# A two-layer streaming encoder: conditioning matmuls issued four together, and up-projection blocks without overlapping columns

## The chip, the cores and the metric

The kernel runs on one core of one Trainium2 chip. The metric is the device time of one launch, in microseconds. TensorE does the matmuls (PE in the profile, PEld its weight loads), VectorE is DVE, ScalarE is ACT, GpSimd is POOL; SyncE (SP) issues all DMAs of this kernel.

## What is computed

One inference step of a two-layer encoder over 1152 rows (1024 of a prompt and 8 x 16 of samples) of 1024 features. Both layers have attention, a feed-forward part with a causal convolution of width 3, and shifts, scales and gates that come from a condition vector `c`:

```python
sc = jax.nn.silu(c)
for l in range(DEPTH):
    ada = (sc @ w_ada[l] + b_ada[l])[:, None, :]
    sh_m, sc_m, g_m, sh_f, sc_f, g_f = jnp.split(ada, 6, axis=-1)
    h = x * (1 + sc_m) + sh_m
    ...
    x = layer_norm(DEEPNORM_ALPHA * x + (1 + g_m) * mix, ln_g[l, 0], ln_b[l, 0])
    h = x * (1 + sc_f) + sh_f
    f, conv_rows = conv_ffn(h, None if prompt else state_conv[l], w_up[l], conv_w[l], conv_b[l], w_down[l])
    ...
    x = layer_norm(DEEPNORM_ALPHA * x + (1 + g_f) * f, ln_g[l, 1], ln_b[l, 1])
```

```python
def conv_ffn(h, prev, w_up, conv_w, conv_b, w_down):
    u = h @ w_up
    ...
    ue = jnp.concatenate([prev.astype(u.dtype), u], axis=1)
    y = conv_b
    for tap in range(CONV_W):
        y = y + conv_w[tap] * ue[:, tap:tap + T]
    a, g = jnp.split(y, 2, axis=-1)
    out = (jax.nn.gelu(g) * a) @ w_down
    return out, ue[:, T:]
```

The convolution goes over positions, so each output position needs the up-projection at its own position and at the two before it.

## The kernel before

**Stages.** `build` runs: the first conditioning product (`ada(0, ...)`), attention of layer 0, the output projection, the feed-forward part of layer 0, and the same three for layer 1. In the trace the first attention lies at about 54 to 430 us, feed-forward layer 0 at 535 to 1340, attention of layer 1 to 2040, feed-forward layer 1 at 2130 to the end.

**Precision.** Every large product is made of three: a matrix is split into a high part rounded to the 32-bit format of TensorE's fast matmul (`float32r`) and a low part, the remainder. `split` (L160) makes the high part with a cast and the low part with a subtraction. Weights come through `wload` (L164): a DMA into one of the two staging buffers `ws`, the cast on ScalarE (L151), the subtraction mostly on GpSimd (L162), into one of four weight slots `wh` and `wl`. `mmT` (L262) does 3 x 8 matmuls for one block of columns, first with the low weight part, then twice with the high one.

**The conditioning products.** `ada(gi, ...)` is a generator that makes one of seven slices of the condition. It has eight steps over the 1024 inputs. A step loads two tiles of 128 x 1024 weights and issues four matmuls (L211) that write the four 32-partition groups of one PSUM bank; `j` 0 and 1 read the first tile, `j` 2 and 3 the second. Each has 32 output rows, so it uses 32 of the array's 128 columns. Slice 0 runs by itself at the start. Slices 1 and 2 run in the background of the first attention, where their weights share the two buffers `ws` with the other weights; slices 3 to 6 run in the background of feed-forward layer 0, from a ring of three buffers of the tile `F`. `wload` calls `step`, which advances the generator.

**The feed-forward part.** For each of 22 slices of 128 features and both halves (`gg` 0 for `a`, 1 for `g`) `up` loads a weight and runs `up_block` for three blocks of rows. `up_block` (L1006) projects a block into one of three PSUM banks (`ub`) and calls `conv`: ScalarE makes the last tap with the bias (L976), VectorE adds the two other taps from the same bank (L979), and for samples GpSimd adds what comes from the state (L994). For `gg` 1 the gelu (L1023, ScalarE), the product with the other half (L1025, GpSimd) and a split follow. The blocks overlap, so that a block's bank holds the columns before it that its taps need:

```python
        UB = ((0, 384), (380, 388), (764, 388))
```

`down` (L1030) multiplies the pairs of slices by the down-projection (L1050), from three other banks, and adds into `acc` on VectorE (L1041). `down_last` (L1054) does the last pair, with the last up-projection's six blocks between the row tiles, and hands each row tile to the normalization.

**What sets the order.** The program is recorded in the order of the Python code, and a list scheduler with a timeline of its own then reorders it, engine by engine, by priorities and by what its timeline says is ready. Two neighbours in the code can so be apart on the engine. Inside an engine the order is then fixed, and each instruction waits for the semaphores of what it needs. A wait on PSUM is kept for a whole bank.

Of the kernel before, what the change touches and what calls it, by code (L numbers as in the profile page):

```python
# [20 lines left out]
BLK = ((0, 384), (384, 384), (768, 384))  # L21
# [67 lines left out]
class Trunk:  # L89
# [101 lines left out]
    def ada(self, gi, bank, ring=None, row=None):  # L191
        nc = self.nc
        ring = ring or self.ws
        ps = self.bank(bank)
# [11 lines left out]
        for k in range(8):  # L206
            w = [ring.next() for _ in range(2)]
            for hf in range(2):
                nc.sync.dma_start(w[hf], self.I["adaw"][gi, k, hf])
            for j in range(4):  # L210
                nc.tensor.matmul(  # L211
                    ps[32 * j : 32 * j + 32, :],
                    self.cT[:, k * 32 : k * 32 + 32],
                    w[j // 2][:, (j % 2) * 512 : (j % 2) * 512 + 512],
                    start=k == 0,
                    stop=k == 7,
                    tile_position=(0, 32 * j),
                )
            yield
        if row is None:  # L220
            row = ring.next()
# [721 lines left out]
    def ffn(self, l, xsrc, xdst, affs):  # L943
        nc, I, O, H = self.nc, self.I, self.O, self.H
# [27 lines left out]

        def conv(ps, cc, bi, y):
            w = lambda i: cw[:, cc, i : i + 1]
            off = 0 if bi == 0 else 4
            nc.scalar.activation(y, ps[:, off : off + 384], AF.Identity, bias=w(3), scale=w(2))  # L976

            def tap(o, u, i):
                nc.vector.scalar_tensor_tensor(o, u, w(i), o, op0=ALU.mult, op1=ALU.add)  # L979

            if bi == 0:
                tap(y[:, 1:384], ps[:, 0:383], 1)
                tap(y[:, 2:384], ps[:, 0:382], 0)
            elif bi == 1:
                tap(y, ps[:, 3:387], 1)
                tap(y, ps[:, 2:386], 0)
            else:
                tap(y[:, 0:256], ps[:, 3:259], 1)
                tap(y[:, 0:256], ps[:, 2:258], 0)
                ys = y[:, 256:384].rearrange("p (s q) -> p s q", q=16)  # L990
                us = ps[:, 260:388].rearrange("p (s q) -> p s q", q=16)
# [13 lines left out]

        def up_block(w, j, gg, bi):  # L1006
            cc = j + 22 * gg
            s0, n = UB[bi]
            ps = self.bank(ub.next())
            self.mmT(w, ps, s0, n)  # L1010
            if gg == 0:
                y = ya[bi] = self.ya.next()
            else:
                y = self.yg.next()
            conv(ps, cc, bi, y)
            if bi == 2:
                uo = self.uo[gg].rearrange("p (j s r) -> p j s r", s=9, r=2)
                src = ps[:, 258:402].rearrange("p (s q) -> p s q", q=16)[:, :, 0:2]
                nc.scalar.copy(uo[:, j % 11], src)
# [319 lines left out]
```

## Time and profile before

| | us |
|---|---|
| median of 3 runs | 2995.66 (2993.42 to 2997.04) |
| the profiled execution, its own time | 2989.15 |
| its span, first to last instruction | 2987.3 |
| mean granted TensorE clock in it | 0.984 |
| up-projection and key matmuls, L267 (8208 of them) | 46% of the chain |
| down-projection matmuls, L1050 | 16% of the chain |
| conditioning matmuls, L211 (224, two records each) | 2% of the chain |

The profile is of one execution. "Busy" is the time in which an engine has an instruction in it; matmuls are pipelined and overlap, so the time that one costs is read from the start of one to the start of the next, and not from its length. "The chain of waits" follows the work that ended last back to what released it. The granted clock is a share of TensorE's full clock.

### The profile page before, as it was taken

Reading aid. Unit: us, or ns where it says so; the run is one execution under the profiler, and the core shown is the slowest. Engines: PE = TensorE matmul, PEld = TensorE weight load, DVE = VectorE, ACT = ScalarE, POOL = GpSimd, SP = SyncE. Lnnn points to the kernel's source line nnn. Section 1 sums busy time; section 2 is a strip of 40 time slices with the busy share of each in tenths; the row PEclk is TensorE's granted clock in tenths of the full one; section 3 lists DMA queues with packets and bytes.
Section 4 is the critical chain, followed back from the end, with each engine's and each line's share of the span. In section 5 each row is a group of like instructions: output and inputs, shape, how many; then the busy total and the mean of one; then the engine's idle time right before and its main releaser. Section 6 shows DMA issues by size and latency. Waiting matters only on the chain.

```text
span 2987.3 us, 43224 instructions
## 1 busy us (share of the span) xinstructions
PE 2863.8 (96%) x16582; PEld 2545.5 (85%) x16582; DVE 1537.3 (51%) x3416; ACT 1145.7 (38%) x2432; POOL 908.0 (30%) x661
## 2 busy tenths in 40 slices
PE   7999889999999999999999999989999999999996
PEld 4886668888888898997999888867899999999995
DVE  4365668424444343358412677766724444444468
ACT  3464643332222222224434666662442222222224
POOL 2122332322222222344561121231432222222253
PEclk9999989999999999999999999999999999999998
DMA  8655353722222222212795467673311111111121
GB/s 299 189 150 160 109 151 113 238 81 77 94 81 86 83 72 99 82 64 103 267 309 165 130 152 195 181 226 118 125 50 38 41 43 46 43 41 40 42 84 74
DMA packets 175535, 353.95 MB, mean 118 GB/s; under 512 B 34632, under 2 KB 91784, under 8 KB 174944
## 3 DMA queue, kind: packets, MB, share of 16 engines
q1 hardware_dynamic: 175328, 351.19, 37.0%
q8 instruction: 130, 2.13, 0.3%
q14 instruction: 77, 0.63, 0.1%
HBM read 285.22 MB, written 75.35 MB: 121 GB/s over the span
## 4 chain that ended last, share of the span: by engine, by line
PE 79%; DVE 8%; DMA 6%; ACT 3%; POOL 2%; issue 2%; SPq 0%; DVEq 0%; ACTq 0%; POOLq 0%
PE PS L267 46%; PE PS L1050 16%; PE PS L279 8%; PE PS L552 2%; PE PS L211 2%; PE PS L533 2%; DMA ws<-in_wo_dram 1%; PE PS L507 1%; DMA F<-in_adaw_dram 1%; DVE F L473 1%; PE PS L510 1%; DMA F<-xd 1%; DVE acc L1110 1%; DMA ws<-oN 1%; POOL wl L162 1%
## 5 line engine op out<-in xcount | busy, mean ns | idle before, releaser
L267 PE MATMUL PS<-H,wh 128*128 128x384 f32 (+1 forms) x5472 | 1045.9, 339 | 0.3 <-DVE H L162 0.3
L267 PEld LDWEIGHTS PS<-H,wh 128*128 128x128 f32 x5472 | 966.6, 188 | 17.5 <-issue 7.5
L162 POOL TENSOR_TENSOR wl<-ws,wh 128x1024 fp32r<-128x1024 f32 x167 | 404.8, 2429 | 751.1 <-ACT wh L151 704.0
L979 DVE SCALAR_TENSOR_TENSOR F<-PS,F 128x256 f32<-128x256 f32 (+2 forms) x704 | 352.9, 512 | 535.7 <-ACT F L976 522.5
L267 PE MATMUL PS<-H,wl 128*128 128x384 f32 (+1 forms) x2736 | 565.1, 343 | 19.6 <-POOL wl L162 7.8
L267 PEld LDWEIGHTS PS<-H,wl 128*128 128x128 f32 x2736 | 486.3, 189 | 53.2 <-issue 18.6
L976 ACT ACTIVATE F<-PS,F 128x384 f32<-128x384 f32 x264 | 177.3, 672 | 751.1 <-PE PS L267 749.6
L1050 PE MATMUL PS<-wh,X 128*128 128x512 f32 x1320 | 412.2, 394 | 10.3 <-DVE acc L1041 4.1
L1041 DVE TENSOR_TENSOR acc<-acc,PS 128x512 f32<-128x512 f32 x324 | 221.4, 685 | 271.6 <-PE PS L1050 271.1
L1025 POOL TENSOR_TENSOR F<-F 128x384 f32<-128x384 f32 x132 | 138.0, 1046 | 649.4 <-ACT F L1023 647.5
L1050 PEld LDWEIGHTS PS<-wh,X 128*128 128x128 f32 x1320 | 245.4, 188 | 64.0 <-issue 6.7
L151 ACT CAST wh<-ws 128x1024 fp32r<-128x1024 f32 x174 | 180.0, 1045 | 154.9 <-PE PS L1050 75.3
L1050 PE MATMUL PS<-wl,X 128*128 128x512 f32 x660 | 216.4, 392 | 0.0
L279 PE MATMUL PS<-wh,H 128*128 128x256 f32 (+1 forms) x936 | 172.5, 314 | 6.3 <-DVE H L162 6.0
L279 PEld LDWEIGHTS PS<-wh,H 128*128 128x128 f32 x936 | 137.3, 195 | 17.0 <-DVE H L162 6.8
L1050 PEld LDWEIGHTS PS<-wl,X 128*128 128x128 f32 x660 | 124.1, 188 | 28.1
L589 POOL TENSOR_TENSOR F<-F,x2att 64x512 f32<-64x512 f32 x62 | 79.4, 1280 | 212.8 <-DVE F L564 171.4
L162 DVE TENSOR_TENSOR X<-F,X 128x384 fp32r<-128x384 f32 x110 | 96.9, 881 | 88.7 <-ACT X L151 88.4
L279 PE MATMUL PS<-x1att,H 128*128 128x512 f32 x504 | 131.8, 402 | 4.9 <-ACT x1att L151 2.7
L533 PE MATMUL PS<-C,F 128*128 128x128 f32 x720 | 118.3, 285 | 17.4 <-DVE wh L539 7.5
L1023 ACT ACTIVATE F<-F 128x384 f32<-128x384 f32 x132 | 69.2, 524 | 143.3 <-DVE F L979 129.0
L279 PEld LDWEIGHTS PS<-x1att,H 128*128 128x128 f32 x504 | 94.7, 190 | 27.8 <-ACT x1att L151 3.4
(211 smaller groups left out, 3477.8 us busy)
## 6 DMA issues: line engine op xcount, KB each, us to landing
ws<-in_wup_dram SPq DMA_DIRECT2D x88, 512.0 KB
F<-in_adaw_dram SPq DMA_DIRECT2D x74, 512.0 KB
ws<-in_wdn_dram SPq DMA_DIRECT2D x44, 512.0 KB
ws<-in_adaw_dram SPq DMA_DIRECT2D x32, 512.0 KB
x1att<-kH SPq DMA_DIRECT2D x60, 256.0 KB
xd<-F SPq DMA_DIRECT2D x27, 512.0 KB
F<-xd SPq DMA_DIRECT2D x27, 512.0 KB
vH<-X SPq DMA_DIRECT2D x40, 256.0 KB
```

Source lines behind the costliest of these rows:

```text
L151: nc.scalar.copy(out, in_)
L162: self.eng(el).tensor_sub(lo, src, hi.bitcast(F32))
L267: self.nc.tensor.matmul(out[:, 0:n], w[a][:, k * 128 : k * 128 + 128], H[:, p, k, s0 : s0 + n], start=i == 0, stop=i == 23)
L279: self.nc.tensor.matmul(out[:, 0:n], H[:, p, j * kn + k, t0 : t0 + 128], w[a][:, k * n : k * n + n], start=i == 0, stop=i == 23,)
L533: nc.tensor.transpose(t[:, m * 128 : m * 128 + 128], p[:, (kt - k0) * 128 : (kt - k0) * 128 + 128], self.ident)
L589: self.eng("v" if last else "p").tensor_mul(on[r, q], on[r, q], rb[r, :])
L976: nc.scalar.activation(y, ps[:, off : off + 384], AF.Identity, bias=w(3), scale=w(2))
L979: nc.vector.scalar_tensor_tensor(o, u, w(i), o, op0=ALU.mult, op1=ALU.add)
L1023: nc.scalar.activation(y, y, AF.Gelu_apprx_tanh)
L1025: nc.gpsimd.tensor_mul(a, y, ya[bi])
L1041: nc.vector.tensor_add(row[:, n], row[:, n], ps)
L1050: nc.tensor.matmul(ps, ac[m][p][:, cs], w[m][q][:, n], start=i == 0, stop=i == 5)
```

## The change

It edits two places.

In `ada` the four matmuls of a step are issued, for every slice but the first, in the order 2, 3, 0, 1. The first of them (`lead`) is ordered as before; the other three get a high priority and an instruction that they may only be issued after the lead. The lead reads the second tile.

In the feed-forward part the three blocks no longer overlap (`BLK`: 0, 384 and 768, 384 columns each). The second and third block are written from column 2 of their bank on, and ScalarE then copies the last two columns of the block before, from that block's bank, into columns 0 and 1. The copy stands behind the matmuls in the code. The offsets in `conv` follow.

```diff
-            for j in range(4):
-                nc.tensor.matmul(
...
+            lead = None
+            for j in (2, 3, 0, 1) if gi else (0, 1, 2, 3):
+                with ExitStack() as es:
+                    if lead is not None:
+                        es.enter_context(self.tc.high_priority())
+                        es.enter_context(self.tc.issue_after(lead))
+                    mm = nc.tensor.matmul(
+                        ps[32 * j : 32 * j + 32, :],
+                        self.cT[:, k * 32 : k * 32 + 32],
+                        w[j // 2][:, (j % 2) * 512 : (j % 2) * 512 + 512],
...
+                if gi and lead is None:
+                    lead = mm.ins
...
-            off = 0 if bi == 0 else 4
+            off = 0 if bi == 0 else 2
...
-                tap(y, ps[:, 3:387], 1)
-                tap(y, ps[:, 2:386], 0)
+                tap(y, ps[:, 1:385], 1)
+                tap(y, ps[:, 0:384], 0)
...
-        UB = ((0, 384), (380, 388), (764, 388))
+        halo = {}
...
-            s0, n = UB[bi]
+            s0, n = BLK[bi]
             ps = self.bank(ub.next())
-            self.mmT(w, ps, s0, n)
+            off = 0 if bi == 0 else 2
+            self.mmT(w, ps[:, off:512], s0, n)
+            if bi:
+                nc.scalar.copy(ps[:, 0:2], halo.pop(cc))
+            if bi < 2:
+                halo[cc] = ps[:, off + 382 : off + 384]
```

Line numbers below 200 stay; in the changed program L211 is L216, L267 is L274, L976 is L983, L979's taps are L986, L1019 is L1031, L1023 is L1035, L1050 is L1062, and the new copy is L1020.

The scheduler sees a different program, so the order moves in many places: on TensorE in the first attention and in both feed-forward layers, not in attention of layer 1. Three places follow. In a row stand the line, the operation, the output and input tiles, the output's shape and, behind an x, how many equal instructions follow each other.

TensorE in feed-forward layer 0, at the end of an up-projection and the start of the down-projections, before. `PS<-F,C` are the conditioning matmuls, `PS<-H,wl` and `PS<-H,wh` the up-projection with the low and high weight parts, `PS<-wh,X_73` and `PS<-wl,X_73` the down-projection.

```order
L267 MATMUL PS<-H,wh 128x388 x16
L211 MATMUL PS<-F,C 32x512 x4
L1050 MATMUL PS<-wh,X_73 128x512 x2
...
L1050 MATMUL PS<-wh,X_73 128x512 x2
L211 MATMUL PS<-F,C 32x512 x2
L267 MATMUL PS<-H,wl 128x384 x8
L1050 MATMUL PS<-wh,X_73 128x512 x2
...
L1050 MATMUL PS<-wh,X_73 128x512 x2
L211 MATMUL PS<-F,C 32x512 x2
L267 MATMUL PS<-H,wh 128x384 x9
```

The same place now:

```order
L274 MATMUL PS<-H,wh 128x384 x16
L216 MATMUL PS<-F,C 32x512 x4
L1062 MATMUL PS<-wh,X_73 128x512 x2
...
L1062 MATMUL PS<-wh,X_73 128x512 x2
L274 MATMUL PS<-H,wl 128x384 x8
L274 MATMUL PS<-H,wh 128x384 x6
L1062 MATMUL PS<-wh,X_73 128x512 x2
...
L1062 MATMUL PS<-wh,X_73 128x512 x2
L216 MATMUL PS<-F,C 32x512 x4
L274 MATMUL PS<-H,wh 128x384 x6
```

Two pairs of conditioning matmuls have become one group of four. Over feed-forward layer 0 the 32 steps stood in 38 groups (two of 1, eleven of 2, one of 3, twenty-one of 4, one of 5, two of 6) and stand in 32 groups of 4; in the first attention the 16 steps stood in 25 groups and stand in 19 (thirteen of 4 and six of 2). The second and third blocks of an up-projection have gone from 388 to 384 columns.

ScalarE in feed-forward layer 1, in the stretch of up-projections, before. `F<-PS,F` is the first activation of a block, `F<-F` the gelu, `wh<-ws` a weight's high part, `X_73<-F` that of a product, `F<-PS 128x18` the copy of the rows that go out as state.

```order
L976 ACTIVATE F<-PS,F 128x384
L1023 ACTIVATE F<-F 128x384
L151 CAST x2ffn_17144<-F 128x384
L976 ACTIVATE F<-PS,F 128x384 x2
L151 CAST wh<-ws 128x1024
L1019 COPY F<-PS 128x18
L976 ACTIVATE F<-PS,F 128x384
```

And now:

```order
L983 ACTIVATE F<-PS,F 128x384
L151 CAST x2ffn_17232<-F 128x384
L1020 COPY PS<-PS 128x2
L983 ACTIVATE F<-PS,F 128x384
L1020 COPY PS<-PS 128x2
L151 CAST wh<-ws 128x1024
L983 ACTIVATE F<-PS,F 128x384
L1031 COPY F<-PS 128x18
```

The copies stand ahead of the activations of the second and third block, and the weight cast has come between the third block's copy and its activation.

TensorE in `down_last` of layer 1, before: the last blocks of the last up-projection and the down-projections around them.

```order
L267 MATMUL PS<-H,wh 128x388 x9
L267 MATMUL PS<-H,wl 128x388 x8
L267 MATMUL PS<-H,wh 128x388 x16
L1050 MATMUL PS<-wh,X_73 128x512 x2
L1050 MATMUL PS<-wl,X_73 128x512 x2
L1050 MATMUL PS<-wh,X_73 128x512 x4
```

And now:

```order
L274 MATMUL PS<-H,wh 128x384 x9
L1062 MATMUL PS<-wh,X_73 128x512 x2
L1062 MATMUL PS<-wl,X_73 128x512 x2
L1062 MATMUL PS<-wh,X_73 128x512 x4
...
L1062 MATMUL PS<-wh,X_73 128x512 x2
L274 MATMUL PS<-H,wl 128x384 x8
L274 MATMUL PS<-H,wh 128x384 x16
```

The last block no longer follows its neighbour directly; it stands behind 18 more down-projection matmuls.

More of the change, by code (lines that the diff above doesn't have):

```diff
@@ L209, in ada @@
                 nc.sync.dma_start(w[hf], self.I["adaw"][gi, k, hf])
-            for j in range(4):
[L211 to L218, printed above, removed]
+            lead = None
[8 more added lines that the diff above has]
+                        w[j // 2][:, (j % 2) * 512 : (j % 2) * 512 + 512],
+                        start=k == 0,
+                        stop=k == 7,
+                        tile_position=(0, 32 * j),
+                    )
+                if gi and lead is None:
+                    lead = mm.ins
             yield
@@ L984, in conv @@
             elif bi == 1:
-                tap(y, ps[:, 3:387], 1)
-                tap(y, ps[:, 2:386], 0)
-            else:
-                tap(y[:, 0:256], ps[:, 3:259], 1)
-                tap(y[:, 0:256], ps[:, 2:258], 0)
+                tap(y, ps[:, 1:385], 1)
+                tap(y, ps[:, 0:384], 0)
+            else:
+                tap(y[:, 0:256], ps[:, 1:257], 1)
+                tap(y[:, 0:256], ps[:, 0:256], 0)
                 ys = y[:, 256:384].rearrange("p (s q) -> p s q", q=16)
-                us = ps[:, 260:388].rearrange("p (s q) -> p s q", q=16)
+                us = ps[:, 258:386].rearrange("p (s q) -> p s q", q=16)
                 tap(ys[:, :, 1:16], us[:, :, 0:15], 1)
```

2 lines of the change are left out of this document (1 added, 1 removed).

## The prediction

> **What bounds the kernel now.** I read the page first: the busy shares, then the chain that ended last.
>
> ```profile
> PE 2863.8 (96%) x16582; PEld 2545.5 (85%) x16582; DVE 1537.3 (51%) x3416; ACT 1145.7 (38%) x2432; POOL 908.0 (30%) x661
> ...
> PE 79%; DVE 8%; DMA 6%; ACT 3%; POOL 2%; issue 2%; SPq 0%; DVEq 0%; ACTq 0%; POOLq 0%
> PE PS L267 46%; PE PS L1050 16%; PE PS L279 8%; PE PS L552 2%; PE PS L211 2%; PE PS L533 2%; DMA ws<-in_wo_dram 1%; PE PS L507 1%; DMA F<-in_adaw_dram 1%; DVE F L473 1%; PE PS L510 1%; DMA F<-xd 1%; DVE acc L1110 1%; DMA ws<-oN 1%; POOL wl L162 1%
> ```
>
> TensorE is busy 96% of the span and holds 79% of the chain. Both edited places, the up-projection matmuls (L267) and the conditioning matmuls (L211), stand on that chain. A share over the span is an average, so next comes the table by stretches: the first attention, then the two feed-forward layers.
>
> ```profile
> 110.00:350.00 240.00, 226.95 (x1586) 184.57 (x1584) 151.99 (x525) 146.05 (x446) 59.86 (x61) 0.97 0.48 144
> 535.00:1340.00 805.00, 802.60 (x4236) 715.07 (x4235) 318.20 (x552) 220.87 (x372) 230.91 (x179) 1.00 0.28 94
> 2130.00:2987.30 857.30, 829.53 (x4339) 776.54 (x4337) 408.81 (x716) 258.36 (x436) 266.59 (x190) 0.99 0.16 52
> ```
>
> The columns are PE, PEld, DVE, ACT and POOL busy, then the granted clock, the DMA share and GB/s. In feed-forward layer 0 TensorE is busy 802.60 of 805 us, in layer 1 829.53 of 857.30 (the rest is the output tail), in the first attention 226.95 of 240. So in the feed-forward layers a nanosecond less per matmul is a nanosecond off the end, while ScalarE has 70% to spare.
>
> **The columns.** Of the three blocks of each up-projection, two had 388 columns and now have 384, from 384-aligned starts in H. I price this from two pieces of the chain and four starts in the timeline.
>
> ```profile
> 1466.63 93.95 PE PS L267 x542
> ...
> 2378.44 39.79 PE PS L267 x226
> ```
>
> ```profile
> 2380.04 1.58 PE L267 MATMUL PS<-H,wl 128*128 128x384 f32 x8
> ...
> 2384.23 1.58 PE L267 MATMUL PS<-H,wl 128*128 128x388 f32 x8
> ...
> 2388.48 1.57 PE L267 MATMUL PS<-H,wl 128*128 128x388 f32 x8
> ...
> 2392.72 1.58 PE L267 MATMUL PS<-H,wl 128*128 128x384 f32 x8
> ```
>
> The first piece is the key projection of attention 1. It runs the same function over exactly the blocks that the change will use, all of 384: 93.95 / 542 = 173.3 ns each. The second is a stretch of three up-projections: 39.79 / 226 = 176.1 ns. By the starts, a 384 block after a 388 one takes 4.19 us and the 388 blocks 4.25 and 4.24. There are 2 layers x 44 projections x 72 = 6336 such matmuls: 6336 x 2.72 ns = 17.2 us (by the starts, 88 x (12.68 - 72 x 0.1733) = 88 x 0.20 = 17.6). Bounds: no gain, if writing the output at column 2 of the bank costs what the four columns did, which no row shows; 17.6 above. I take 17.2, since only that output offset differs from the row.
>
> The Trainium skill, "TensorE: Matmul & The Clock Gate", section "Back-to-back issue gap", gives a warm gap of N/2.4 + 2.5 ns, so that four columns would be worth 1.67 ns; as an estimate by that page, 4224 matmuls would save 7.0 us, and the whole sum would come to 19.6 us in place of 29.8. The trace does not agree on the level: it has 173.3 ns at 384 columns where the page's formula has 162.5.
>
> **The conditioning matmuls.** Four matmuls of one step write four different 32-row groups of one bank and run side by side when they stand together. The timeline of layer 0 has them both ways (the trace writes each as two records).
>
> ```profile
> 730.16 1.68 PE L267 MATMUL PS<-H,wl 128*128 128x384 f32 x8
> ...
> 743.03 1.07 PE L211 MATMUL PS<-F,C 128*32 128x512 f32 x8
> 744.03 1.68 PE L267 MATMUL PS<-H,wl 128*128 128x384 f32 x8
> ...
> 762.21 1.05 PE L211 MATMUL PS<-F,C 128*32 128x512 f32 x4
> 763.19 1.66 PE L267 MATMUL PS<-H,wl 128*128 128x384 f32 x8
> ```
>
> ```profile
> 590.53 1.90 PE L211 MATMUL PS<-F,C 128*32 128x512 f32 x10
> 592.36 1.69 PE L267 MATMUL PS<-H,wl 128*128 128x388 f32 x8
> ```
>
> All four hold TensorE for 1.00 us (743.03 to 744.03), two alone for 0.98. So a pair costs what a four costs. What counts is the number of interruptions. One costs 13.87 (730.16 to 744.03, with one) - 12.68 (2380.04 to 2392.72, without) = 1.19 us. In layer 0 the order has 38 groups before and 32 now: 6 x 1.19 = 7.1 us. Three groups had five or six matmuls and took a second pass, 1.83 - 1.00 = 0.83 us: 2.5 us. Together 9.6 us, on an engine without idle time there. The lead of a four now waits for the second weight tile, and the other three stand right behind it; the rows for what such a wait costs are these, of layer 0 and of the first attention:
>
> ```profile
>   DMA F<-in_adaw_dram: 2.4, 1
> ```
>
> ```profile
>   DMA ws<-in_adaw_dram: 4.0, 4
> ```
>
> In layer 0 TensorE waited once, 2.4 us, for the tile that the first step needs; I leave that where it is. In the first attention the 16 steps stood in 25 groups and stand now in 19 (three steps are still split): 6 x 0.98 = 5.9 us of TensorE time, in a stretch with 13 us of idle time in which other waits end last. I take 4 us. SP's queue holds the same DMAs as before; the weight loads (L209) move a few places past the small score and output DMAs and past one query weight. Bounds: a gain of 9.9 (5.9 and all of the 4.0 of DMA waits), and a loss of 10: the two weight buffers `ws` are shared with the query weights, a four holds both until it has run, and if each of 16 steps waited 1.0 us more (the mean of those four waits), 16 - 5.9 would be lost. Queued behind such a lead are the score and transpose matmuls, for which VectorE waits.
>
> **The halo copies.** 176 copies of 2 columns are new on ScalarE, before the first activation (L976) of the second and third block. A copy waits for its own block's last matmul and, for the bank it reads, for the block before.
>
> ```profile
> L976 ACT ACTIVATE F<-PS,F 128x384 f32<-128x384 f32 x264 | 177.3, 672 | 751.1 <-PE PS L267 749.6
> ```
>
> ```profile
> L1019 ACT COPY F<-PS x88: 149/174/243, 551.2 to 2953.2; 128x18 f32<-128x18 f32 x88
> ```
>
> The nearest row for its price is the other small copy out of PSUM (L1019), 0.174 us: 176 x 0.174 = 30.6 us more on ScalarE, which waited 749.6 us for these very matmuls. How long a block keeps its bank is read from the second block of the stretch above, which ends at 2388.48, and from the rows of its neighbours:
>
> ```profile
> 2388.68 0.67 ACT L976 ACTIVATE F<-PS,F 128x384 f32<-128x384 f32 x1 [1.52 <-PE PS L267]
> ```
>
> ```profile
> 2389.38 1.27 DVE L979 SCALAR_TENSOR_TENSOR F<-PS,F 128x384 f32<-128x384 f32 x2
> ```
>
> ```profile
>   DVE F L979: 1.5, 1
> ```
>
> ```profile
> PEld PS L267 <- POOL wl L162: 13.1, 8, 5.0
> ```
>
> The activation starts 0.20 us after the block, and the taps end at 2390.65, 2.2 us after it. With the copy and its hand-over (0.17 + 0.20) that is 2.6 us; TensorE comes back to this bank two blocks later, 8.5 us after. So 5.9 us of slack cover the copy, and I cost it at 0; without cover it would be 30.6 (176 x 0.174). TensorE's waits for the taps were 1.5 us in all of layer 1. Queued behind a waiting copy on ScalarE are the block's own activation, for which VectorE's taps and then GpSimd's product wait, and in places a weight cast (L151), whose lower half GpSimd makes next; for such halves TensorE waited 13.1 us in the whole program, so they mostly come well ahead of their use. One place has less slack: in `down_last` a block goes into the bank from which the block before it takes its halo, so TensorE must wait for that copy, 0.4 us by the numbers above, four times, unless other matmuls stand between. The order puts down-projection matmuls between; I take 1 us of loss, bounds 0 and 2. In the output tail TensorE waits already:
>
> ```profile
> 2954.08 0.73 PE L1050 MATMUL PS<-wh,X 128*128 128x512 f32 x2 [0.89 <-DVE C L1086]
> ...
> 2959.81 0.50 PE L1050 MATMUL PS<-wh,X 128*128 128x512 f32 x1 [2.25 <-DVE C L1086]
> ```
>
> The last up block now stands in the middle of the down-projections there, with 3.1 us of such waits around it. I count neither gain nor loss, up to 3 us each way.
>
> **Sum.** 17.2 + 9.6 + 4 - 1 = 29.8 us. The profiled execution took 2989.15 us (span 2987.3 and 1.85 around it) and becomes 2959.4. The median of the runs shown is 2995.66, 6.5 above it; the same difference gives 2965.9, so 2966.
>
> **Rivals.** (1) *The columns are worth less.* If a matmul's time went with its columns alone, four would be worth 173.3 / 384 x 4 = 1.8 ns, 7.6 us for 4224; then the sum is 20.2 and the time 2975. If the output offset costs as much as it saves, 2983. The Trainium skill, "TensorE: Matmul & The Clock Gate", section "Back-to-back issue gap", speaks for this side, with one cycle a column. For it stands that only one kind of row, at one alignment, shows 173.3. Against it, that row reads the same addresses.
> (2) *The fours wait for their second tile in the first attention*, losing 10 in place of gaining 4: 2980. For it: both `ws` buffers are held, and the DMA share is 0.48 there. Against: 16 steps in 240 us are 15 us apart.
> (3) *Slower: TensorE becomes bound by the halo copy.* If banks come free late because copies stand behind other work on ScalarE, every second and third block waits. It decides from 30.8 / 176 = 0.175 us a block; at 0.37 (the copy and its hand-over) the loss is 65.1 and the time 3030. For it speaks that a copy waits at the head of an in-order queue, against it the 5.9 us of slack.
> (4) *The fours do not run as fours on the chip*, or something slips between: the columns and the loss of 1 stay, 2979.5. The order speaks against it.
>
> **Chances.** The forecast 0.68, rival 1 0.16, rival 2 0.07, rival 3 0.06, rival 4 0.03. The forecast's own range is 2957 to 2975: 2957 with the attention's upper bound and a kinder tail, 2975 with no gain in the attention and both losses full. Rival 1 ends at 2983, rivals 2 and 4 lie below it. So 2954 to 2984. A measurement of this kernel can tell about 0.2%, 6 us, from no change. Faster by more than that: 0.68 + 0.16, 0.05 of rival 2 and 0.02 of rival 4, 0.91. Within it: 0.02 of rival 2, 0.01 each of rivals 3 and 4, 0.04. Slower: 0.05 of rival 3.
>
> **What would show it.** In the profile after: L267 in attention 1 and in the layers at one mean interval, a piece of 226 of them at 39.2 us in place of 39.79; the same starts 4.16 apart. L211 in layer 0 in 32 runs of eight records, each about 1.0 us. L1019's neighbour, the 2-column copy, at 0.17 us x176, and no row of TensorE that waits for it or for L979 beyond 2 us. The prediction is wrong if the interval stays at 176, if L211 shows DMA waits of over 10 us, or if TensorE's idle time in the layers grows by more than 5 us.

## The result, and the profile after

The changed kernel took 3005.91 us (median of 9 runs, 2997.72 to 3010.45), the kernel before on the same chip 2993.79 (9 runs). The ratio is 1.0033, 95% interval 1.0022 to 1.0044: slower by about 10 us, where 2966 was predicted. The profiled execution took 3007.52 us, its span 3005.7, at a mean granted clock of 0.974 in place of 0.984.

The page after, busy shares and the chain that ended last:

```profile
PE 2859.9 (95%) x16582; PEld 2548.1 (85%) x16582; DVE 1563.2 (52%) x3416; ACT 1162.4 (39%) x2608; POOL 904.0 (30%) x661
...
PE 70%; DVE 7%; ACT 3%; DMA 2%; issue 2%; POOL 2%; SPq 0%; DVEq 0%; ACTq 0%; POOLq 0%
```

TensorE is a little less busy in a longer span. The steady stretches show what was predicted of the columns. First a piece of the chain, then four starts from the timeline:

```profile
2391.52 39.37 PE PS L274 x227
```

```profile
2393.30 1.55 PE L274 MATMUL PS<-H,wl 128*128 128x384 f32 x8
...
2397.45 1.55 PE L274 MATMUL PS<-H,wl 128*128 128x384 f32 x8
...
2401.61 1.55 PE L274 MATMUL PS<-H,wl 128*128 128x384 f32 x8
...
2405.78 1.55 PE L274 MATMUL PS<-H,wl 128*128 128x384 f32 x8
```

39.37 / 227 = 173.4 ns, and the blocks start 4.16 us apart: output from column 2 on costs nothing. So the loss lies elsewhere. The table by stretches has the same windows as before:

```profile
110.00:350.00 240.00, 224.04 (x1566) 182.95 (x1565) 149.94 (x514) 142.56 (x437) 59.49 (x61) 0.96 0.47 142
535.00:1340.00 805.00, 799.15 (x4278) 718.21 (x4277) 343.01 (x570) 230.37 (x457) 236.11 (x182) 1.00 0.28 96
2130.00:3005.70 875.70, 837.37 (x4375) 781.61 (x4373) 427.10 (x719) 272.86 (x534) 273.03 (x193) 0.98 0.16 53
```

The last window spans 18 us more, and TensorE is idle 38.3 us in it where it was 27.8. Windows of equal length are too coarse to say where. I therefore cut the execution at the same instructions in each kernel (us from start to start; the kernels in the three columns on the right are experiments that follow):

| stretch | before | changed | old blocks in last slice | old blocks in first two and last | halo by taps |
|---|---|---|---|---|---|
| first output projection to first down-projection, layer 0 | 208.1 | 208.5 | 206.6 | 195.7 | 195.2 |
| from there to the last slice, layer 0 | 767.9 | 754.5 | 754.3 | 759.6 | 758.0 |
| last slice, layer 0 | 61.3 | 73.1 | 64.4 | 64.6 | 68.1 |
| end of output projection to first down-projection, layer 1 | 63.7 | 75.5 | 75.1 | 62.8 | 55.0 |
| from there to the last slice, layer 1 | 728.6 | 719.2 | 719.2 | 723.3 | 729.1 |
| last slice, layer 1 | 53.3 | 66.5 | 54.0 | 55.2 | 57.9 |

The two long stretches gain 13.4 and 9.4. Three short ones give back 11.8, 11.8 and 13.3: the last slice of each layer, and the start of feed-forward layer 1. (Where up- and down-projections are put shifts some time between a start and the stretch behind it, so these two are read together.) By the same cuts, TensorE's idle time in these three grew by 20.7 us, and it lost 11.8 us more to a lower clock; the other 4.4 are mostly work that moved into the start of layer 1 from the stretch behind it. Outside the table the changed kernel loses 6.9 us up to the first output projection, which starts at 396.55 in place of 389.70, and 1.0 in attention of layer 1, and gains 4.0 behind the last matmul.

**The start of feed-forward layer 1.** TensorE before, then after. The first block of a projection is 384 wide in both; H's third block of columns is still being made here.

```profile
2135.46 1.63 PE L267 MATMUL PS<-H,wl 128*128 128x384 f32 x8 [1.52 <-DVE F L979]
2136.93 2.94 PE L267 MATMUL PS<-H,wh 128*128 128x384 f32 x16
2139.70 1.04 PE L867 MATMUL PS<-C,F 128*128 128x128 f32 x8
2140.50 1.66 PE L267 MATMUL PS<-H,wl 128*128 128x388 f32 x8
2142.00 2.99 PE L267 MATMUL PS<-H,wh 128*128 128x388 f32 x16
2144.82 1.58 PE L267 MATMUL PS<-H,wl 128*128 128x384 f32 x8
```

```profile
2142.76 2.34 PE L274 MATMUL PS<-H,wl 128*128 128x384 f32 x8 [1.83 <-ACT PS L1020]
2144.90 3.69 PE L274 MATMUL PS<-H,wh 128*128 128x384 f32 x15
2148.43 1.03 PE L874 MATMUL PS<-C,F 128*128 128x128 f32 x8
2149.22 0.42 PE L274 MATMUL PS<-H,wh 128*128 128x384 f32 x1
2153.52 2.82 PE L274 MATMUL PS<-H,wl 128*128 128x384 f32 x8 [3.88 <-ACT H L151]
```

Before, five blocks stand ahead of the first that needs H's third part: two of the first projection, two of the second (2135.46 and 2140.50), one of a third (2144.82). After, three do. The second block of the second projection would go into the bank that holds the halo for the third block of the first. That copy (L1020) stands behind the third block's matmuls, which wait for H. So nothing is left to put there, and TensorE waits 3.88 us for the cast of H. The wait of 1.83 us ahead of it was 1.52 before, for the taps alone.

The waits cost more than their length. The granted clock is the third number from the end of a row in the table by windows:

```profile
2142.00:2143.00 1.00, 0.23 (x1) 0.27 (x2) 0.90 (x5) 0.49 (x2) 0.00 (x0) 1.00 0.00 0
2143.00:2144.00 1.00, 1.00 (x6) 1.00 (x6) 1.00 (x2) 0.33 (x1) 0.12 (x1) 0.71 0.09 16
2144.00:2145.00 1.00, 1.00 (x5) 1.00 (x4) 0.94 (x2) 0.00 (x0) 1.00 (x1) 0.50 0.00 0
2145.00:2146.00 1.00, 1.00 (x5) 1.00 (x4) 0.00 (x0) 0.00 (x0) 1.00 (x1) 0.50 0.00 0
2146.00:2147.00 1.00, 1.00 (x5) 1.00 (x4) 0.72 (x1) 0.00 (x0) 0.25 (x1) 0.58 0.00 0
```

Behind the wait the clock is halved for some 3.4 us: 0.29 + 0.50 + 0.50 + 0.42 = 1.71 us lost. The transposes at 2148.43, on which the cast of H depends, come later by that. The Trainium skill, "TensorE: Matmul & The Clock Gate", section "What's actually happening", has a window of 3413 ns, and half the rate after one that was idle. The trace agrees with the length and the rate, but no whole idle window was needed here: a wait of 1.83 us was enough.

**The last slice.** A block goes here into the bank from which the block before it takes its halo. The second blocks, in layer 0 after, on ScalarE and then on TensorE:

```profile
1372.23 0.52 ACT L1035 ACTIVATE F<-F 128x384 f32<-128x384 f32 x1 [0.60 <-DVE F L986]
1374.16 0.51 ACT L151 CAST X<-F 128x384 fp32r<-128x384 f32 x1 [1.40 <-POOL F L1037]
1374.57 0.15 ACT L1020 COPY PS<-PS 128x2 f32<-128x2 f32 x1
```

```profile
1374.78 2.43 PE L274 MATMUL PS<-H,wl 128*128 128x384 f32 x8 [3.28 <-ACT PS L1020]
```

The copy took 0.15 us and could have run 0.2 us after the block. It stood on ScalarE behind the gelu and the cast of another block, and that cast waited 1.40 us for GpSimd. TensorE waited 3.28 us, and in layer 1 at the same place 1.72. For the very last block the scheduler put down-projection matmuls between, 12 in layer 0 and 18 in layer 1. In the output tail the last up block so came later against the rest, and TensorE waits for its result:

```profile
PE PS L1062 <- DVE x2ffn L162: 9.0, 1, 9.0
```

Before, no wait behind the last up block was longer than 2.25 us. The copies over the whole execution:

```profile
L1020 ACT COPY PS<-PS 128x2 f32<-128x2 f32 x176 | 25.6, 145 | 407.2 <-PE PS L274 388.2
```

Summed over windows of 1 us, TensorE is idle 145.1 us (123.1 before) and loses 60.5 us to a lower clock while busy (33.8 before). The profiled span grew by 18.4 us: 22.0 of idle time and 26.7 of clock, less 30.3 us by which TensorE's busy time, reckoned at full clock, fell. The prediction's terms for the matmuls themselves were 17.2, 9.6 and, in the first attention, 5.9, together 32.7. So the work was saved nearly as forecast, and waits and clock took back more than all of it.

### The profile page after: what moved, and what is told of

It is laid out like the page before. It is cut to its first block, busy times and chain, and to the rows that moved or that the text cites. A ratio compares the mean times of both kernels' runs of the same rounds, so it can differ in the third digit from the quotient of the medians.

```text
span 3005.7 us, 43456 instructions
## 1 busy us (share of the span) xinstructions
PE 2859.9 (95%) x16582; PEld 2548.1 (85%) x16582; DVE 1563.2 (52%) x3416; ACT 1162.4 (39%) x2608; POOL 904.0 (30%) x661
## 4 chain that ended last, share of the span: by engine, by line
PE 70%; DVE 7%; ACT 3%; DMA 2%; issue 2%; POOL 2%; SPq 0%; DVEq 0%; ACTq 0%; POOLq 0%
PE PS L274 40%; PE PS L1062 16%; PE PS L286 7%; PE PS L559 1%; PE PS L540 1%; PE PS L216 1%; DVE acc L1122 1%; PE PS L514 1%; DVE F L480 1%; ACT F L784 1%; DMA oSD<-C 1%; DVE F L946 1%; PE PS L517 1%; PE PS L874 0%; POOL acc L1121 0%
## 5 line engine op out<-in xcount | busy, mean ns | idle before, releaser
L274 PE MATMUL PS<-H,wh 128*128 128x384 f32 x5472 | 1051.8, 337 | 0.3 <-DVE H L162 0.3
L274 PEld LDWEIGHTS PS<-H,wh 128*128 128x128 f32 x5472 | 964.2, 189 | 21.3 <-issue 5.4
L274 PE MATMUL PS<-H,wl 128*128 128x384 f32 x2736 | 561.8, 342 | 38.0 <-POOL wl L162 9.8
L986 DVE SCALAR_TENSOR_TENSOR F<-PS,F 128x256 f32<-128x256 f32 (+2 forms) x704 | 352.7, 511 | 463.5 <-ACT F L983 453.1
L274 PEld LDWEIGHTS PS<-H,wl 128*128 128x128 f32 x2736 | 485.9, 190 | 71.7 <-issue 15.7
L1062 PE MATMUL PS<-wh,X 128*128 128x512 f32 x1320 | 420.1, 395 | 8.5 <-DVE acc L1053 3.2
L1062 PEld LDWEIGHTS PS<-wh,X 128*128 128x128 f32 x1320 | 245.1, 188 | 60.1 <-issue 9.2
L983 ACT ACTIVATE F<-PS,F 128x384 f32<-128x384 f32 x264 | 177.9, 674 | 243.7 <-PE PS L274 240.0
L1062 PE MATMUL PS<-wl,X 128*128 128x512 f32 x660 | 217.1, 394 | 0.0
L162 DVE TENSOR_TENSOR X<-F,X 128x384 fp32r<-128x384 f32 x110 | 125.4, 1140 | 117.1 <-ACT X L151 116.9
L1020 ACT COPY PS<-PS 128x2 f32<-128x2 f32 x176 | 25.6, 145 | 407.2 <-PE PS L274 388.2
L286 PE MATMUL PS<-wh,H 128*128 128x256 f32 (+1 forms) x936 | 173.1, 315 | 7.7 <-DVE H L162 7.2
L286 PEld LDWEIGHTS PS<-wh,H 128*128 128x128 f32 x936 | 137.3, 194 | 18.8 <-DVE H L162 7.8
L1062 PEld LDWEIGHTS PS<-wl,X 128*128 128x128 f32 x660 | 124.6, 189 | 28.5
L540 PE MATMUL PS<-C,F 128*128 128x128 f32 x720 | 119.2, 287 | 18.4 <-DVE wh L546 8.0
L286 PE MATMUL PS<-x1att,H 128*128 128x512 f32 x504 | 133.2, 405 | 1.6 <-ACT x1att L151 1.4
L1035 ACT ACTIVATE F<-F 128x384 f32<-128x384 f32 x132 | 69.3, 525 | 145.7 <-DVE F L986 140.8
```

The lines of the kernel that those rows point to most:

```text
L162: self.eng(el).tensor_sub(lo, src, hi.bitcast(F32))
L274: self.nc.tensor.matmul(out[:, 0:n], w[a][:, k * 128 : k * 128 + 128], H[:, p, k, s0 : s0 + n], start=i == 0, stop=i == 23)
L286: self.nc.tensor.matmul(out[:, 0:n], H[:, p, j * kn + k, t0 : t0 + 128], w[a][:, k * n : k * n + n], start=i == 0, stop=i == 23,)
L540: nc.tensor.transpose(t[:, m * 128 : m * 128 + 128], p[:, (kt - k0) * 128 : (kt - k0) * 128 + 128], self.ident)
L1062: nc.tensor.matmul(ps, ac[m][p][:, cs], w[m][q][:, n], start=i == 0, stop=i == 5)
```

## The experiments

My theory after the result, A: the halo copy holds a bank until the next block's matmuls are over, which takes away the scheduler's freedom where a feed-forward part begins and in its last slice. The rivals: B, the conditioning edit disturbs the first attention; C, the columns bring less than I took; D, the number of small copies costs; E, a copy at the head of ScalarE's queue keeps the casts behind it. All results follow, with the ratio to the kernel before on the same chip. Not all kernels ran on one chip, so rows are best compared by their ratios; microseconds under or above the kernel before are worked out from the ratio:

| kernel | median us (runs) | ratio, 95% interval |
|---|---|---|
| fours alone | 2985.67 (12) | 0.9990 (0.9978 to 1.0003) |
| blocks alone | 3012.28 (6) | 1.0074 (1.0056 to 1.0091) |
| both, no halo | 2976.25 (6) | 0.9950 (0.9932 to 0.9968) |
| halo through SBUF | 2993.42 (12) | 1.0005 (0.9993 to 1.0017) |
| old blocks in the last slice | 2993.42 (12) | 1.0003 (0.9991 to 1.0015) |
| halo copy on VectorE | 3007.19 (6) | 1.0046 (1.0031 to 1.0060) |
| halo by taps | 2983.58 (9) | 0.9967 (0.9955 to 0.9978) |
| fours in layer 0's feed-forward only | 2979.43 (6) | 0.9953 (0.9936 to 0.9969) |
| old blocks in first two and last slices | 2975.76 (5) | 0.9942 (0.9930 to 0.9954) |
| fours, lead on the first tile | 2977.57 (6) | 0.9946 (0.9932 to 0.9960) |
| taps, fours in feed-forward only | 2980.43 (6) | 0.9958 (0.9945 to 0.9971) |
| the same, saved by VectorE | 2977.77 (5) | 0.9954 (0.9942 to 0.9965) |
| old blocks in three slices, fours in feed-forward only | 2971.42 (6) | 0.9923 (0.9910 to 0.9936) |
| changed, fours in feed-forward only | 3004.33 (6) | 1.0037 (1.0024 to 1.0050) |
| old blocks in three slices, no fours | 2985.79 (8) | 0.9978 (0.9966 to 0.9991) |
| four banks, changed | 3091.72 (4) | 1.0335 (1.0315 to 1.0355) |
| four banks, before | 3086.95 (5) | 1.0312 (1.0296 to 1.0328) |
| four banks, changed, fours in feed-forward only | 3089.45 (4) | 1.0325 (1.0304 to 1.0345) |

### Each edit alone

Fours alone: the diff of `ada`, nothing else.

> Only the conditioning edit; the up-projection blocks stay as before (overlapping, 388 columns, no halo copy). Theory A (the halo copy holds the bank of the block before until the next block's matmuls are over, so that blocks can no longer be put in another order where a stage begins or ends; the loss of the change comes from there): this kernel gains, about 8 to 10 us in feed-forward layer 0 and a loss of up to 5 in the first attention, so 4 to 9 us under the kernel before. Theory B (the loss comes from the conditioning edit: the order of the first attention is disturbed, and what it gives late is late everywhere): 8 us or more above the kernel before, with the loss in place before 540 us.

Blocks alone: the rest of the diff.

> Only the blocks of 384 columns and the halo copy; the conditioning matmuls stay as before. Theory A: slower than the kernel before by 10 to 25 us: 17 us gained in the steady stretches, and 35 or more given back at the start of feed-forward layer 1 (12), in the last down-projection of layer 0 (12) and of layer 1 (13). Theory B: 15 to 17 us faster than the kernel before.

Fours alone are 3.0 us under the kernel before (6.6 under to 0.9 above), blocks alone 22 us above it (17 to 27). Rival B falls as the main cause: the loss is in the blocks. By the profiles, TensorE's busy time at full clock is 15.0 us less with the fours alone (9.6 + 5.9 = 15.5 forecast) and 14.2 us less with the blocks alone (17.2 forecast).

### Without the halo, and with the halo through SBUF

```diff
...
-            self.mmT(w, ps[:, off:512], s0, n)
-            if bi:
-                nc.scalar.copy(ps[:, 0:2], halo.pop(cc))
...
+            self.mmT(w, ps, s0, n)
...
```

> Both edits, but no halo at all: each of the three blocks of an up-projection starts at column 0 of its bank, the copies are gone, and the convolution of the second and third block leaves out the two taps that reach into the block before (its first two columns get the last tap alone). Theory A: without the copy the blocks are free again, and the sum of the prediction comes true: 20 to 30 us under the kernel before. Theory B: about as the changed kernel, or at best 10 us under it (2996 to 3006). Theory C (the columns bring less than I took): within 10 us of the kernel before.

```diff
+        self.hs = fa.ring(2, 2)
...
             if bi < 2:
-                halo[cc] = ps[:, off + 382 : off + 384]
+                halo[cc] = self.hs.next()
+                nc.scalar.copy(halo[cc], ps[:, off + 382 : off + 384])
```

> Both edits, but each block's last two columns are first copied to a small buffer in SBUF right behind its matmuls, and from there to the next block's bank; a bank is free when its taps and that copy are done, whatever the next block does. 176 more copies on ScalarE of 0.15 us. Theory A: the order of blocks at the start of feed-forward layer 1 is that of the kernel before again, and the time 10 to 25 us under it. Theory D (the copies cost by their number, on ScalarE's queue, and not by the bank that they hold): as slow as the changed kernel or slower, 3006 or more.

Without a halo the kernel is 15 us under the kernel before (10 to 20): the loss in the three stretches is gone but for 2.7 and 2.0 us in the last slices, as A has it, but 20 to 30 were expected. Against fours alone on the same chip the 384 columns are worth 2985.67 - 2976.25 = 9.4 us by the medians and 12.0 by the two ratios, within some 6. That is less than 17.2, so rival C seems to have a part, of a size that these runs do not settle. Through SBUF the loss of the change is gone and no more; 10 to 25 under was expected, so this expectation failed. TensorE at the start of layer 1 had its five blocks ahead again. But one copy still waits for the next block's matmuls, and other work stands behind it on ScalarE (first row; behind it a cast, three activations and two small copies, then the copy L1033 out of PSUM); TensorE waits for the last of these:

```profile
2157.43 0.16 ACT L1021 COPY PS<-F 128x2 f32<-128x2 f32 x1 [5.62 <-PE PS L274]
...
2161.75 0.17 ACT L1033 COPY F<-PS 128x18 f32<-128x18 f32 x1 [1.37 <-DVE F L987]
```

```profile
2161.97 2.90 PE L274 MATMUL PS<-H,wl 128*128 128x384 f32 x8 [3.89 <-ACT F L1033]
```

So E is real in this kernel. (Its buffer in SBUF has two places, where the kernel with taps below has four. A save that has to wait for a free place would be one more coupling; no run here separates it.) Whether E is at work in the changed kernel, the next runs ask.

### The place, the queue, the taps

```diff
...
-                        up_block(wu[gg], NFF - 1, gg, bi)
+                        up_block(wu[gg], NFF - 1, gg, bi, 4)
```

The last argument 4 takes the blocks of the kernel before (388 columns, offset 4, no copy).

> The changed kernel, with the overlapping blocks (388 columns, no halo copy) back in the last up-projection of each layer only, the one whose six blocks stand between the last down-projections. Theory A (a bank is held by the halo copy until the next block's matmuls are over): the 24 us that these two places lost come back, and the loss of 12 at the start of feed-forward layer 1 stays: 4 to 16 us under the kernel before. If these places lose for another reason (the blocks of 384 columns, the fours before them): still 8 us or more above the kernel before.

```diff
-                nc.scalar.copy(ps[:, 0:2], halo.pop(cc))
+                nc.vector.tensor_copy(ps[:, 0:2], halo.pop(cc))
```

> The changed kernel with the halo copy on VectorE in place of ScalarE, everything else as it is. The bank is held as long as before. Theory A alone (the bank that is held): as the changed kernel, 8 to 18 us above the kernel before. Theory E (the copy waits at the head of ScalarE's queue, and the casts behind it that make H and the weights come late): the start of feed-forward layer 1 gets 4 to 8 us back in each layer, so -2 to 8 us above the kernel before.

```diff
+        self.hs = fa.ring(4, 2)
...
+            if p is not None:
+                tap(y[:, 0:2], p, 0)
+                tap(y[:, 0:1], p[:, 1:2], 1)
...
+            p = halo.pop(cc, None)
+            if bi < 2:
+                h = halo[cc] = self.hs.next()
+                nc.scalar.copy(h, ps[:, 382:384])
...
```

> Both edits, but the halo goes to no bank: ScalarE saves a block's last two columns to SBUF right behind the block's matmuls, and VectorE adds their share to the first two outputs of the next block in two small operations of 2 and 1 columns. Nothing on ScalarE waits for the next block's matmuls, and no bank waits for another block. Theories A and E together: 8 to 16 us under the kernel before, within 4 us of the kernel without a halo. Theory D (the number of small operations costs): at or above the kernel before.

Old blocks in the last slice alone bring the time back to that of the kernel before. In the table by stretches the two last slices recover 8.7 and 12.5 us of 11.8 and 13.3, the start of layer 1 stays at 75.1. The whole gained less than I expected: 0.9 us above the kernel before (2.7 under to 4.5 above), where 4 to 16 under was expected. The copy on VectorE does not change the total (14 us above): another queue with the same bank held does not help, so E alone isn't the cause. The start of layer 1 stays at 75.6 with it; only the last slice of layer 0 gets 4.5 us back (68.6), the place where the copy stood behind other work on ScalarE, so E may have a part there. The taps, which leave neither a bank held nor a queue waiting, came out in the range of A and E together: 9.9 us under (6.6 to 13.5). But that is 5 short of the kernel without a halo, where 4 was allowed, and the last slices keep 6.8 and 4.6 us of the loss. D falls as the main cause, with 352 more operations on VectorE.

```diff
...
-                up_block(w, j, gg, bi)
+                up_block(w, j, gg, bi, 4 if j < 2 else 2)
...
```

> The changed kernel, with the overlapping blocks back in three places of each layer: the first two slices of features (where a feed-forward part begins, its H still comes in) and the last. The 19 slices between keep 384 columns and the halo copy. If the held bank costs only where the scheduler needs to put other blocks between (theory A): the start of feed-forward layer 1 gets back its 11 to 12 us, so 8 to 14 us under the kernel with the overlapping blocks in the last slice alone, and 6 to 14 us under the kernel before. If the start loses for another reason: as that kernel, at the time of the kernel before.

This is the sharpest test of the place. 19 of 22 slices keep 384 columns and the halo copies, in the steady stretch; the kernel is 17.4 us under the kernel before (13.8 to 20.9), 18 better than with the last slice alone. The start of layer 0, which I had not counted among the losses, gains too: 206.6 us become 195.7. Some is taken back in the steady stretches, 5.3 and 4.1 us, so start and steady stretch together gain 5.6 us in layer 0 and 8.2 in layer 1.

### A fourth bank

```diff
-        ub = Ring([0, 1, 2])
-        db = Ring([3, 4, 5])
+        ub = Ring([0, 1, 2, 3])
+        db = Ring([4, 5])
```

> The changed kernel, with four PSUM banks for the up-projection and two for the down-projection in place of three and three. Every halo copy stays. Theory A (a bank held until the next block's matmuls are over): with a fourth bank two blocks can stand between, the two lossy places recover, and the kernel is 8 to 20 us faster than the changed one, so between 2 above and 10 us under the kernel before, if the two banks of the down-projection cost nothing (the control tells). If the copies themselves cost: as the changed kernel, 10 to 12 above.

> The kernel before, with four banks for the up-projection and two for the down-projection; the control for the changed kernel with the same banks. Its own blocks need no bank of their neighbours: within 4 us of the kernel before, if two banks are enough for the down-projection; slower by what they are short of otherwise.

> The changed kernel with four banks for the up-projection, and with the fours in feed-forward layer 0 only. Theory A and the 0 to 9 us that fours in the first attention cost so far: 0 to 9 us faster than the changed kernel with four banks and all fours. It would have to come under 2971 to beat the kernel with overlapping blocks in the first two and last slices.

Two banks for the down-projection cost 93 us in the control, where I had allowed 4, so the totals can't decide. The order moves and TensorE waits for weights:

```profile
PE PS L267 <- POOL wl L162: 51.1, 18, 4.9
```

The stretches can be read, against the control, which has the same banks: the start of layer 1 takes 66.9 us against 66.1 (with three banks 75.5 against 63.7), the last slices 4.1 and 4.5 us more than the control's (with three banks 11.8 and 13.3). Every copy is still there. With one more bank the loss at the start is gone and two thirds of that in the last slices: it is the bank, as A says. The third run adds nothing: 2 us less than with all fours, within its interval.

### The fours of the first attention

```diff
-            for j in (2, 3, 0, 1) if gi else (0, 1, 2, 3):
+            for j in (2, 3, 0, 1) if gi > 2 else (0, 1, 2, 3):
...
-                if gi and lead is None:
+                if gi > 2 and lead is None:
```

> The kernel before, with the fours only for slices 3 to 6 (feed-forward layer 0); slices 1 and 2, in the first attention, stay in pairs, and the blocks stay as before. If the fours of the first attention gain 4 us as the prediction has it: 3 to 5 us slower than the kernel with all fours. If they lose there (both buffers of the weights held by a four until it has run): up to 5 us faster than that one.

> Only the conditioning edit (as in the kernel with fours alone), but for slices 1 and 2, in the first attention, the four begins with the matmuls of the first weight tile (order 0, 1, 2, 3, each behind the lead), so that the lead waits for the first tile and the third matmul for the second. If the loss of the fours there comes from the wait for the second tile at the lead alone: up to 3 us faster than with the other order. If it comes from the held buffers and from the moved order in general: within 4 us of the kernel with fours alone (5 us under the kernel before), and above the kernel with fours in feed-forward layer 0 only (14 under).

Fours in the feed-forward only: 14.1 us under the kernel before, against 3.0 with all fours. So in the attention fours cost 11 us, where I had counted a gain of 4 (the expectation allowed 5). TensorE's waits there, with all fours:

```profile
PE PS L216 <- DMA ws<-in_adaw_dram: 6.9, 8, 1.8
```

4.0 us before. And it goes on behind them: in the output projection and at the start of the feed-forward part TensorE waits 4.9 us once (L286, for VectorE's half of H) and 3.6 us once (L274, for VectorE's taps), where the kernel before has no single wait over 2.4. The kernel with the lead on the first tile does not tell what I meant it to: by the trace its attention has 28 groups, as the kernel before has by its trace (25 in the order of its program), and not the 19 of the kernels with fours there. The lead on the first tile left the pairs apart. It took 2977.57, as the kernel without fours there. My expectation for it failed, and it is one more kernel without fours in the attention.

### Putting the parts together

> The halo by taps from SBUF (9.5 us under the kernel before together with all fours) and the fours in feed-forward layer 0 only (13.6 under, 9 better than all fours). If the two add: 16 to 22 us under the kernel before. If the fours of the attention and the halo got in each other's way rather than each costing by itself: 9 to 12 under.

> As the kernel with taps from SBUF and fours in feed-forward layer 0 only, but VectorE, which reads the same bank for its taps, saves the two columns in place of ScalarE. If the queue of ScalarE still costs something (casts behind 176 small copies): 1 to 4 us faster than with ScalarE. If neither queue is a limit: within 3 us of it.

> The overlapping blocks in the first two and the last slice, 384 columns with the halo copy in the 19 between, and fours in feed-forward layer 0 only. If what was found adds (16.7 us under the kernel before with all fours, and 9 for the attention's fours): 22 to 27 us under the kernel before. If the parts overlap, as they did in the kernels with taps (12 in place of 18): 15 to 19 under.

> The changed kernel, but with the fours in feed-forward layer 0 only; slices 1 and 2 in pairs as before. If the fours of the first attention cost 9 us in the change too: 1 to 6 us above the kernel before (the changed kernel is 10 to 12 above). If their cost and that of the held banks are one and the same (both make the start of feed-forward layer 0 late): 9 us or more above.

> The overlapping blocks in the first two and the last slice, 384 columns with the halo copy in the 19 between, and no fours at all. 19 of 22 slices keep the gain. If the columns are worth the 17.2 us of the prediction: 19/22 of it, 13 to 16 us under the kernel before. If they are worth what four columns cost by the number alone (7.6): 5 to 8 us under. What the intervals of TensorE show (176.2 to 173.8 ns) lies between, 13.

With taps the parts do not add (12.6 us under, 16 to 22 expected); which engine saves the columns makes no difference that can be told. With old blocks in three slices they do: 6.6 us (2.7 to 10.2) for the blocks alone and 14.1 for the fours alone make 20.7, and the two together are 23 us under (19 to 27), the fastest kernel here. In its windows TensorE is idle 1.5 us in feed-forward layer 0 and 24.5 in layer 1 with its tail:

```profile
535.00:1340.00 805.00, 803.47 (x4311) 722.60 (x4312) 346.42 (x569) 229.36 (x450) 239.63 (x182) 1.00 0.28 96
2130.00:2970.90 840.90, 816.44 (x4281) 762.53 (x4279) 409.81 (x699) 263.33 (x506) 261.53 (x186) 0.99 0.15 51
```

In the changed kernel itself pairs in the attention save nothing (1.0037 against 1.0033). What the attention's fours cost is thus 11 us with the old blocks, 5.7 with old blocks in three slices, 2.7 with taps and none in the change, each within some 5 or 6 us. Why it depends on the rest was not settled.

## Why the prediction was wrong

**The step that failed** is the one on the halo copies: "So 5.9 us of slack cover the copy, and I cost it at 0", with "I take 1 us of loss, bounds 0 and 2" for `down_last` and "I count neither gain nor loss" for the tail. The price was right (0.145 us measured, 0.174 taken), and so was the slack, for the stretch that it was read from: in the steady part of layer 1 no row of TensorE waits for L1020. But "TensorE comes back to this bank two blocks later" holds only there. Where the scheduler had put blocks of other projections between, the copy forbids it. I looked for the time that the copy takes and not for the order that it rules out. The three places lost 36.9 us by the profile (11.8, 11.8, 13.3): 20.7 of idle time, 11.8 of half clock behind waits, and work that moved. By the ratios the changed kernel is 25 us slower than the one without a halo, where the forecast had 1.

**The columns** had the right mechanism, and the term was too large. In the piece that I priced by, the interval fell to 173.4 ns as predicted (227 of them in 39.37 us). Over the whole steady stretch of layer 1 the mean from one up-projection matmul to the next fell from 176.1 to 173.9 ns: 2.2 ns in place of 2.72, which is 14 us for 6336 matmuls. The busy time of blocks alone says the same, 14.2 us. In time the columns were worth less, 9.4 to 12 us (no halo against fours alone), or 6.6 in 19 of 22 slices, against 17.2; rival 1 had 7.6. What makes the difference between busy time and time was not settled.

**The fours in layer 0's feed-forward** were right: 32 groups in place of 38, each of eight records and 1.00 us (one of them at 604.06 to 605.06). 9.6 was predicted, 14.1 (9 to 19) measured for them alone.

**The fours in the first attention** had the wrong sign, a gain of 4 with bounds of 9.9 and -10. Rival 2 names what the trace shows, the wait for the second tile (L216's DMA waits are 8.1 us in the changed kernel, 4.0 before), but says nothing of the waits behind it. Its size, a loss of 10, is near the 11 us that the fours cost there with the old blocks.

**Rival 3**, slower by the halo copy, had 6 chances in 100. Its mechanism, banks that come free late, is the one that happened, but not as a price for every block: it is paid at two kinds of places. **Rival 4** is out; the fours run as fours.

Of the signs that I named, the interval, the starts, the eight records and the price of the copy came as forecast and looked like success. Two told otherwise. TensorE's idle time in the layers grew by more than 5 us, 10.5 in the last window alone; and one row of TensorE waited 3.28 us for the copy, where none was to wait more than 2.

## What to carry to other kernels

An operation that reads one buffer only after work on another has ended couples the two, and a list scheduler then loses the orders that filled its gaps. Ask of such an edit which orders it forbids, and look where a stage begins and ends, not in the steady stretch; there the cheap remedy was to keep the old form in 3 of 22 slices. And a gain that is read from one interval should be checked on a whole run of the loop, and then in time: 17.2 us by the interval were 14 by the mean of the whole stretch, and 9 to 12 in time. Work that an engine saves becomes time only where its waits do not grow.

## What the runs showed of the hardware

A wait of 1.83 us was followed by half clock for 3.4 us, at a loss of 1.71 us; the one of 1.72 us at 2939.98 was followed by none. Where a wait lies matters. In the changed kernel's trace the clock changes only at times that are a whole multiple of 3.413 us apart (2143.42, 2146.84, 2153.66, 2157.08 and, 226 steps on, 2928.49). The wait of 1.83 us lay within one such step, from 2140.01 to 2143.42; the one of 1.72 lay across the border at 2938.73, 0.47 us before it and 1.25 behind. In the two feed-forward layers of this trace (in layer 0 from the first down-projection on, in layer 1 from the first up-projection on) the six steps at full clock in which TensorE idled 1.83 us or more were followed by half clock, and none with 1.61 us or less was. In the traces of the other kernels with three banks the two cases overlap between 1.58 and 1.90 us, so an idle half of a step is about what it takes. The steps do not begin with the program: counted from its first instruction, the first border lies at 3.27 us in this trace and at 2.54 in that of the kernel before. Whether a wait near that size costs clock is therefore partly luck.

Over the profiled execution the change cost more by the lower clock (26.7 us) than by the idle time itself (22.0).
